# Turning the softmax weights of a cross-decoder in 32x32 squares on VectorE and through DRAM scratch, in place of TensorE transposes

## The chip, the cores and the metric

One NeuronCore of a Trainium2 chip runs the whole kernel. The metric is the time of one execution in microseconds (us) on the device.

## The reference, cut to what matters

The kernel computes a two-layer decoder trunk on 256 tokens of width 2048, all in float32. Layer one is a gated linear attention mixer and a gated convolutional FFN. Layer two is the cross-decoder: it makes keys and values from the output of layer one, attends to them and adds another FFN. With 256 tokens and blocks of 256 keys there is one block, so each query attends causally to all keys up to its own:

```python
kv = rms_norm(x, norm_w) @ w_kv
k, v = jnp.split(kv, 2, axis=-1)
k = rms_norm(k.reshape(B, S, H, Dh), k_norm_w)        # 16 heads of 128
v = v.reshape(B, S, H, Dh)
...
q = (rms_norm(q, q_norm_w) * (Dh ** -0.5)).transpose(0, 2, 1, 3)
...
s_own = jnp.einsum('bhqd,bhkd->bhqk', q_c, k_own)
s_own = s_own + bias_table[:, rel_bucket(dist_own)][None]
s_own = jnp.where(dist_own >= 0, s_own, -jnp.inf)
p = jax.nn.softmax(scores, axis=-1)
o = jnp.einsum('bhqk,bhkd->bhqd', p_own, v_own)
```

The softmax weights of a head are made with queries on partitions and keys along the free dimension. The product with the values needs them with keys on partitions, so they have to be turned.

## The kernel before

**Weights.** The kernel is a long row of matrix products against float32 weights that pass through once. `WeightStream` loads them in chunks of 128x2048 (1 MB) into three buffers `wraw` on SyncE's queue (L112). Each chunk is worked off in two halves of 128x1024: ScalarE rounds a half to `whi` (L132), VectorE subtracts to get the rest `wlo` (L133), and TensorE multiplies with both. There are four buffers each for `whi` and `wlo`; splits are issued two to three halves ahead. The next load is issued when a `wraw` buffer is free, that is after the L133 of the second half of an earlier chunk.

**Steps and jobs.** Each half is one `step()`. Side work is put in a list with `after(n, job)`, which lets `job` run before the n-th step from now. A scheduler then orders each engine's instructions; `tc.issue_after(x)` keeps an instruction behind x in that order. Each engine, SyncE's and GpSimd's DMA queues among them, goes through its instructions in order.

**The cross-decoder.** Q, K and V are each projected in four groups g of 8 halves (`gemm_tok`, L357 and L360), four heads per group; chunks of K are `w_kk`, of V `w_kv`. In the text, half n counts from the first half of K, so K has halves 0 to 31 and V 32 to 63. After a K group, `head_norm` squares and normalizes it (L917, L918 on ScalarE; L920, L921, L925 on VectorE; the power L923 on GpSimd) and `features` turns it for the scores (L933 on TensorE, L936 and L938 on ScalarE, L939 on VectorE). Then, per head, `softmax(hd)` multiplies the scores (L949, L951), adds the bias and takes the maximum (L958), exponentiates (L960) and scales (L962, L964). The three blocks of a head, queries 0 to 127 against keys 0 to 127 and queries 128 to 255 against both key tiles, stand side by side in one tile of 128x384. `turn(hd)` transposes the three blocks on TensorE into PSUM (L971, tile `pT`) and splits 256 columns of the result into `whi`-like and `wlo`-like parts for the exact product (`split`, L382 and L383) and copies the other 128 (L977). `values` multiplies with V (L434).

**Other users of the queues there.** `make_ahead` loads later weights (L314, `ahead<-w_dn`) on SyncE, adds and subtracts their parts on VectorE (L311, L312) and stores them on GpSimd's queue (L321, `tsum<-ahead`). `bias_rows` writes and reads a small scratch for the bias (`bscr`, L909). `turn_h` and `last_down` write and read `hscr`.

The jobs of a K group before the change:

```python
        for i in range(4):
            after(5 + i, lambda i=i, g=g: softmax(4 * g + i))
            after(7 + i, lambda i=i, g=g: turn(4 * g + i))
```

Of the kernel before, what the change touches and what calls it, by code (L numbers as in the profile page):

```python
# [8 lines left out]
F32 = mybir.dt.float32  # L9
# [16 lines left out]
MH = 16  # L26
# [119 lines left out]
def trunk(ctx: ExitStack, tc: tile.TileContext, xT, cst, msk, w1p, w2a, w_k, w_qa, w_v2, w_v, w_g, w_go,  # L146
          w_up0, w_dn0, w_kk, w_kv, w_mq, w_mo, w_up1, w_dn1, rel, onehot, out):
    nc = tc.nc
    V, A, T = nc.vector, nc.scalar, nc.tensor
# [9 lines left out]
    dram = ctx.enter_context(tc.tile_pool(name="dram", bufs=1, space=DRAM))  # L159

    def slot(shape, dt, name):
        return big.tile(shape, dt, name=name, tag="slot")
# [4 lines left out]
    def bank(name, shape):  # L167
        return mis_ps.tile(list(shape), F32, name=name, tag="bank")

    ws = WeightStream(tc, raw, parts)  # L170
# [4 lines left out]
    for layer, todo in enumerate(ahead):  # L175
        t = dram.tile([len(todo), 128, 2048], F32, name=f"tsum{layer}")
# [55 lines left out]
    ident = mk[:, 0:128]  # L232
# [70 lines left out]
    def after(steps, job):  # L303
        later.append((cur[0] + steps, job))
# [43 lines left out]
    def gemm_tok(xs, groups=1):  # L348
        out_ = [acc_ps.tile([128, 2, 512], F32, name="acc") for _ in range(groups)]
        for q0 in range(0, KT, 2):  # L350
            for ps in out_:
                hi, lo = step()
                for ks in ((0,), (1,)) if cur[0] < 3 and groups > 1 else ((0, 1),):
                    tiles_ = [(q0 + k, t, k * 512) for k in ks for t in range(2)]
                    for x0 in (0, S):
                        for kt, t, c in tiles_:
                            T.matmul(ps[:, t, :], xs(kt)[:, x0 + 128 * t:x0 + 128 * t + 128], hi[:, c:c + 512],  # L357
                                     start=kt == 0 and x0 == 0, stop=False)
                    for kt, t, c in tiles_:
                        T.matmul(ps[:, t, :], xs(kt)[:, 128 * t:128 * t + 128], lo[:, c:c + 512],  # L360
                                 start=False, stop=kt == KT - 1)
        ws.prefetch(cur[0])
        return out_ if groups > 1 else out_[0]
# [4 lines left out]
    def both(ps, name):  # L368
        t = temp(name)
        A.copy(t, ps[:, :, S:])  # L370
        V.tensor_add(t, t, ps[:, :, :S])
        return t
# [8 lines left out]
    def split(dst_hi, dst_lo, src):  # L381
        A.copy(dst_hi, src)  # L382
        V.tensor_sub(dst_lo, src, dst_hi.bitcast(F32))  # L383
# [37 lines left out]
    def v_out(v, ps, n):  # L421

        r0, r1 = (n.col[:, t:t + 1] for t in range(2))
        A.activation(v[0][:, 0, :], ps[:, 0, :], AF.Copy, scale=r0)
        V.scalar_tensor_tensor(v[0][:, 1, :], ps[:, 0, :], r0, v[0][:, 0, :].bitcast(F32),
                               op0=OP.mult, op1=OP.subtract)
        A.activation(v[1], ps[:, 1, :], AF.Copy, scale=r1)
# [80 lines left out]
    for hd in range(GH):  # L508
        ps = gemm(xs, KT)
        rstd = nrm.rstd  # L510
        k = both(ps, "k")
        V.tensor_mul(k, k, bc(rstd))
        b = bcum[hd]
# [64 lines left out]
    for hd in range(GH):  # L578
        ps = gemm(xs, KT)
        q = both(ps, "q")  # L580
# [11 lines left out]
    for hd in range(GH):  # L592
        for c in range(2):
            ps = gemm(xs, KT)
            g = both(ps, "g")
# [317 lines left out]
    def head_norm(ps, name):  # L913
        t_, sq = slot([128, 2, 512], F32, name), slot([128, 2, 512], F32, "hsq")
        for t in range(2):
            r = n_q.col[:, t:t + 1]
            A.activation(sq[:, t, :], ps[:, t, :], AF.Square, scale=r)  # L917
            A.activation(t_[:, t, :], ps[:, t, :], AF.Copy, scale=r)  # L918
        ss = small.tile([128, 8], F32, name="ss")
        V.tensor_reduce(ss, sq.rearrange("p t (h d) -> p (t h) d", d=128), axis=AX.X, op=OP.add)  # L920
        V.tensor_scalar(ss, ss, 1.0 / 128, EPS, op0=OP.mult, op1=OP.add)  # L921
        rr = small.tile([128, 8], F32, name="rr")
        nc.gpsimd.tensor_tensor(rr, ss, mhalf, op=OP.pow)  # L923
        u = t_.rearrange("p t (h d) -> p (t h) d", d=128)
        V.tensor_mul(u, u, rr[:, :, None].to_broadcast([128, 8, 128]))  # L925
        return t_

    def features(t_, c, f, scale, c0):

        tp = bank("tr", (128, 2, S))  # L930
        for i in range(2):
            for t in range(2):
                T.transpose(tp[:, i, 128 * t:128 * t + 128],  # L933
                            t_[:, t, (2 * c + i) * 128:(2 * c + i + 1) * 128], ident)
        whole, halves_ = f[0][:, 2 * c:2 * c + 2, :], f[1][c]
        A.activation(whole, tp[:, :, :128], AF.Copy, scale=scale)  # L936
        hi, lo = halves_[:, :, 0, :], halves_[:, :, 1, :]
        A.activation(hi, tp[:, :, c0:], AF.Copy, scale=scale)  # L938
        V.scalar_tensor_tensor(lo, tp[:, :, c0:], scale, hi.bitcast(F32), op0=OP.mult, op1=OP.subtract)  # L939

    qf, kf, ox = [], [], []
    pts = [None] * MH
    p0s, p1s = [], []

    def softmax(hd):
        (q0, q1), (k0, k1) = qf[hd // 4], kf[hd // 4]
        q1, k1 = q1[hd // 2 % 2][:, hd % 2], k1[hd // 2 % 2][:, hd % 2]
        sp = bank("s", (128, 384))
        T.matmul(sp[:, 0:128], q0[:, hd % 4, :], k0[:, hd % 4, :], start=True, stop=True)  # L949
        for i, (a, b) in enumerate(((0, 0), (0, 1), (1, 0))):  # L950
            T.matmul(sp[:, 128:384], q1[:, a, :], k1[:, b, :], start=i == 0, stop=i == 2)  # L951
        s = temp("s", (128, 384))
        st = small.tile([128, 4], F32, name="st")
        bt = bias[hd // 4][:, hd % 4, :]
        for t, (c0, c1) in enumerate(((0, 128), (128, 384))):
            n = c1 - c0
            rev = bass.AP(tensor=bt.tensor, offset=bt.offset + n - 1, ap=[bt.ap[0], [-1, n]])
            V.tensor_tensor_reduce(s[:, c0:c1], sp[:, c0:c1], rev, -1.0, 3.0e38, OP.add, OP.min,  # L958
                                   st[:, t:t + 1])
            A.activation(s[:, c0:c1], s[:, c0:c1], AF.Exp, bias=st[:, t:t + 1], scale=-1.0,  # L960
                         accum_out=st[:, 2 + t:3 + t])
        V.reciprocal(st[:, 2:4], st[:, 2:4])  # L962
        for t, (c0, c1) in enumerate(((0, 128), (128, 384))):
            V.tensor_scalar(s[:, c0:c1], s[:, c0:c1], st[:, 2 + t:3 + t], None, op0=OP.mult)  # L964
        pts[hd] = s

    def turn(hd):
        s = pts[hd]
        tp = bank("pT", (128, 384))
        for c in range(3):  # L970
            T.transpose(tp[:, 128 * c:128 * c + 128], s[:, 128 * c:128 * c + 128], ident)  # L971
        if hd % 8 == 0:
            p1s.append(slot([128, 8, 128], F32, "p1"))
        if hd % 2 == 0:
            p0s.append(slot([128, 2, 2, S], F32R, "p0"))
        split(p0s[-1][:, hd % 2, 0], p0s[-1][:, hd % 2, 1], tp[:, :256])
        A.copy(p1s[-1][:, hd % 8], tp[:, 256:])  # L977

    def values(v, p):
        op = bank("o", (128, 2, S))  # L980
        for i in range(2):
            hd = 2 * p + i
            p0 = p0s[p][:, i]
            mix(op[:, i, :], v, (hd % 4) * 128, p0[:, 0], p0[:, 1], p1s[hd // 8][:, hd % 8])
        o = slot([128, 2, 2 * S], F32R, "ox")
        split(o[:, :, :S], o[:, :, S:], op)
        ox.append(o)
# [7 lines left out]
    for g in range(4):  # L995
# [5 lines left out]
        f = (q8[:, g % 2 * 4:g % 2 * 4 + 4], (q1[:, 0:2], q1[:, 2:4]))  # L1001
# [4 lines left out]
    for g in range(4):  # L1006
        ps = gemm_tok(xs)
        t_ = head_norm(ps, "k")
        if g % 2 == 0:
            k8 = slot([128, 8, 128], F32, "k0")  # L1010
        f = (k8[:, g % 2 * 4:g % 2 * 4 + 4], [slot([128, 2, 2, S], F32R, f"k1{c}") for c in range(2)])
        kf.append(f)
        for c in range(2):
            after(3 + c, lambda t_=t_, c=c, f=f: features(t_, c, f, kqw, 0))
        for i in range(4):
            after(5 + i, lambda i=i, g=g: softmax(4 * g + i))
            after(7 + i, lambda i=i, g=g: turn(4 * g + i))
    for g in range(4):
        ps = gemm_tok(xs)
        if g % 2 == 0:  # L1020
            vm1 = slot([128, 2, 512], F32, "vm1")
        v = (slot([128, 2, 512], F32R, "vm0"), vm1[:, g % 2, :])
        v_out(v, ps, n_q)
        for c in range(2):
            after(1 + c, lambda v=v, p=2 * g + c: values(v, p))
# [116 lines left out]
```

## Time and profile before

| | us |
|---|---|
| median of 3 runs (2206.11 to 2206.84) | 2206.62 |
| the profiled execution, its own time | 2206.03 |
| span of its profile | 2204.2 |
| TensorE (PE) busy | 2197.5 |
| VectorE (DVE) busy | 1760.4 |
| ScalarE (ACT) busy | 1319.0 |
| GpSimd (POOL) busy | 88.5 |

PE is TensorE's matmul, PEld its weight load, SP SyncE; a "q" behind an engine's name is its queue of issued DMAs and waits. In rows of groups the last part gives busy time and the mean time of one in ns, then the idle time of the engine just before them and what ended it. Rows of the timeline start with start and length in us. Rows of windows give stretch, length, then busy time and number of instructions of PE, PEld, DVE, ACT and POOL, the granted clock of TensorE, the busy share of the 16 DMA engines and GB/s. DMA rows give the number of issues, KB each and the median us from issue to landing. Rows of waits give total us, times and the longest. Rows of queues give packets, MB and the share of the 16 engines' span that they took.

### The profile page before, as it was taken

To read this page: it belongs to the slowest core of one execution; us is meant where nothing else is said; L and a number is where in the kernel's file an instruction comes from. 1 tells how busy PE (TensorE), PEld (TensorE's weight loads), DVE (VectorE), ACT (ScalarE), POOL (GpSimd) and SP (SyncE) were. 2 spreads that over 40 slices of the span, in tenths; PEclk is the share of its full clock that TensorE was granted. 3 is DMA by queue.
4 is the path that set the end of the run, shared out by engine and by line. 5 is a ranking of instruction groups with operands and counts; after the bars stand their busy time and mean duration, and the time that the engine had idled before them with its cause. 6 is when DMAs were issued, how large, how long until landed. Compare 5 with 4: busy or idle time off the path is not lost.

```text
span 2204.2 us, 31059 instructions
## 1 busy us (share of the span) xinstructions
PE 2197.5 (100%) x11721; PEld 1899.7 (86%) x11721; DVE 1760.4 (80%) x2539; ACT 1319.0 (60%) x1848; POOL 88.5 (4%) x142
## 2 busy tenths in 40 slices
PE   9999999999999999999999999999999999999999
PEld 7889888888888888888888888888888888888887
DVE  6676877888888887877777777678888888878887
ACT  6655654656556565666656665446655665556565
POOL 0000000000000000000011100000000000000000
PEclk9999999999999999999999999999999999999999
DMA  7675678777777776887768666677777777878995
GB/s 288 211 264 206 235 272 300 265 266 274 271 270 268 278 273 216 296 326 298 279 239 301 243 219 244 224 265 265 267 272 273 273 269 278 290 258 314 321 374 207
DMA packets 91385, 592.41 MB, mean 269 GB/s; under 512 B 10673, under 2 KB 11201, under 8 KB 28514
## 3 DMA queue, kind: packets, MB, share of 16 engines
q1 hardware_dynamic: 75762, 512.69, 65.3%
q0 software_dynamic: 14896, 77.15, 9.1%
q8 instruction: 92, 1.51, 0.3%
q10 hardware_dynamic: 576, 0.58, 0.1%
q14 instruction: 59, 0.48, 0.1%
HBM read 522.99 MB, written 67.40 MB: 268 GB/s over the span
## 4 chain that ended last, share of the span: by engine, by line
PE 99%; DMA 0%; ACT 0%; DVE 0%; SPq 0%; issue 0%
PE acc L342 40%; PE acc L344 21%; PE acc L736 14%; PE acc L357 10%; PE p L736 6%; PE acc L360 5%; PE sT L548 0%; DMA wraw<-w_v 0%; PE tr L933 0%; PE s L951 0%; PE pT L971 0%; PE z L454 0%; PE oT L434 0%; PE s L949 0%; PE o L434 0%; PE hT L800 0%
## 5 line engine op out<-in xcount | busy, mean ns | idle before, releaser
L132 ACT CAST whi<-wraw 128x1024 fp32r<-128x1024 f32 (+1 forms) x786 | 798.5, 1020 | 633.4 <-PE acc L342 302.6
L133 DVE TENSOR_TENSOR wlo<-wraw,whi 128x1024 fp32r<-128x1024 f32 (+1 forms) x786 | 921.4, 1184 | 284.6 <-ACT whi L132 103.5
L342 PE MATMUL acc<-xw,whi 128*128 128x512 f32 x3328 | 796.4, 391 | 0.0
L342 PEld LDWEIGHTS acc<-xw,whi 128*128 128x128 f32 x3328 | 611.4, 188 | 117.5
L344 PEld LDWEIGHTS acc<-xw,wlo 128*128 128x128 f32 x3328 | 427.2, 191 | 16.2
L344 PE MATMUL acc<-xw,wlo 128*128 128x256 f32 x3328 | 433.5, 283 | 0.0
L736 PE MATMUL acc<-whi,hid 128*128 128x512 f32 x596 | 173.9, 390 | 0.0
L133 DVE TENSOR_TENSOR wlo<-ahead,whi 128x1024 fp32r<-128x1024 f32 x92 | 112.2, 1224 | 38.8 <-ACT whi L132 23.3
L357 PE MATMUL acc<-whi,xkv 128*128 128x512 f32 x512 | 132.7, 393 | 0.0
L736 PEld LDWEIGHTS acc<-whi,hid 128*128 128x128 f32 x596 | 111.5, 188 | 22.8
L357 PE MATMUL acc<-whi,xw 128*128 128x512 f32 x512 | 129.7, 393 | 1.4 <-ACT whi L132 1.4
L132 ACT CAST whi<-ahead 128x1024 fp32r<-128x1024 f32 x92 | 96.1, 1054 | 56.4 <-PE p L736 43.4
L736 PE MATMUL p<-whi,hid 128*128 128x512 f32 x386 | 124.8, 390 | 0.0
L357 PEld LDWEIGHTS acc<-whi,xw 128*128 128x128 f32 x512 | 95.2, 188 | 22.2 <-ACT whi L132 2.3
L357 PEld LDWEIGHTS acc<-whi,xkv 128*128 128x128 f32 x512 | 94.4, 188 | 18.2
L685 ACT ACTIVATE au<-up,cs 128x256 f32<-128x256 f32 x176 | 96.0, 593 | 7.9 <-DVE up L681 7.8
L687 DVE SCALAR_TENSOR_TENSOR au<-up,cs,au 128x255 f32<-128x255 f32 x176 | 83.4, 481 | 20.6 <-ACT au L685 20.5
L736 PE MATMUL acc<-wlo,hid 128*128 128x512 f32 x298 | 97.2, 389 | 0.0
L736 PE MATMUL acc<-whi,comb 128*128 128x512 f32 x320 | 95.6, 389 | 0.0
L736 PEld LDWEIGHTS p<-whi,hid 128*128 128x128 f32 x386 | 72.5, 188 | 15.1
L689 DVE SCALAR_TENSOR_TENSOR au<-up,cs,au 128x254 f32<-128x254 f32 x176 | 79.9, 478 | 0.0
L370 ACT COPY up<-acc 128x512 f32<-128x512 f32 x88 | 51.6, 586 | 46.4 <-PE acc L344 45.5
(267 smaller groups left out, 2199.0 us busy)
## 6 DMA issues: line engine op xcount, KB each, us to landing
wraw<-w_up SPq DMA_DIRECT2D x176, 1024.0 KB, 5.1
ahead<-w_dn SPq DMA_DIRECT2D x53, 1024.0 KB, 9.3
tsum<-ahead POOLq DMA_DIRECT2D x53, 1024.0 KB, 7.7
ahead<-tsum SPq DMA_DIRECT2D x46, 1024.0 KB, 6.5
wraw<-w_dn SPq DMA_DIRECT2D x53, 768.0 KB, 6.1
wraw<-w_dn SPq DMA_DIRECT2D x35, 1024.0 KB, 5.4
wraw<-w_g SPq DMA_DIRECT2D x16, 1024.0 KB, 5.3
wraw<-w_go SPq DMA_DIRECT2D x16, 1024.0 KB, 6.6
```

Source lines behind the costliest of these rows:

```text
L132: nc.scalar.copy(hi[:, a:b], src[:, a:b])
L133: self.low = nc.vector.tensor_sub(lo[:, a:b], src[:, a:b], hi[:, a:b].bitcast(F32))
L342: T.matmul(ps[:, b, :], two[i][0][:, c:c + 128], xs(kt), start=kt == 0, stop=False)
L344: T.matmul(ps[:, b, :S], two[i][1][:, c:c + 128], xs(kt)[:, :S], start=False, stop=kt == kts - 1)
L357: T.matmul(ps[:, t, :], xs(kt)[:, x0 + 128 * t:x0 + 128 * t + 128], hi[:, c:c + 512], start=kt == 0 and x0 == 0, stop=False)
L360: T.matmul(ps[:, t, :], xs(kt)[:, 128 * t:128 * t + 128], lo[:, c:c + 512], start=False, stop=kt == KT - 1)
L370: A.copy(t, ps[:, :, S:])
L685: A.activation(au[:, i, :], t[:, i, :], AF.Identity, bias=col(cb + n), scale=col(cw + 2 * 2 * FT + n))
L687: V.scalar_tensor_tensor(au[:, i, 1:], t[:, i, :S - 1], col(cw + 2 * FT + n), au[:, i, 1:], op0=OP.mult, op1=OP.add)
L689: V.scalar_tensor_tensor(au[:, i, 2:], t[:, i, :S - 2], col(cw + n), au[:, i, 2:], op0=OP.mult, op1=OP.add)
L736: T.matmul(p[n], x[xi], w[wi][:, 512 * f:512 * f + 512], start=n not in begun, stop=left[n] == 0)
```

## The change

`turn` no longer uses TensorE. VectorE transposes the 128x384 tile in squares of 32x32, each in its own place. Four DMAs on SyncE's queue, one for each 32 partitions, write the squares to a DRAM scratch `turned`, each to the place that its square has in the transposed matrix, in runs of 32 numbers (128 bytes). One DMA on GpSimd's queue reads the head's three transposed blocks back into SBUF, 3 runs of 512 bytes on each partition. The split and the copy move into a job of their own, `weights(hd)`, four steps after `turn`, and read the tile from SBUF. The writes are ordered behind the last weight load that was issued, and the transpose behind the last L133. `turn`'s tile now comes from the pool of general slots, not from PSUM.

```diff
+    turned = dram.tile([MH, 12, 32, 128], F32, name="turned")
+
     def turn(hd):
-        s = pts[hd]
-        tp = bank("pT", (128, 384))
-        for c in range(3):
-            T.transpose(tp[:, 128 * c:128 * c + 128], s[:, 128 * c:128 * c + 128], ident)
+
+        t = slot([128, 2, 384], F32, "pT")
+        with tc.issue_after(ws.low.ins):
+            V.transpose(t[:, 0], pts[hd])
+        to = turned[hd].rearrange("f b (m a) -> m b f a", a=32)
+        for m in range(4):
+            with tc.issue_after(ws.load.ins):
+                nc.sync.dma_start(to[m], t[32 * m:32 * m + 32, 0].rearrange("b (f a) -> b f a", a=32))
+        nc.gpsimd.dma_start(t[:, 1].rearrange("k (j q) -> k j q", j=3),
+                            turned[hd].rearrange("(j f) b q -> (f b) j q", f=4))
+        pts[hd] = t[:, 1]
+
+    def weights(hd):
+        tp = pts[hd]
         if hd % 8 == 0:
             p1s.append(slot([128, 8, 128], F32, "p1"))
         if hd % 2 == 0:
...
             after(5 + i, lambda i=i, g=g: softmax(4 * g + i))
             after(7 + i, lambda i=i, g=g: turn(4 * g + i))
+            after(11 + i, lambda i=i, g=g: weights(4 * g + i))
```

With the lines that the change adds, the transpose stands at L973 of the changed kernel, the writes at L977, the read at L978 and the copy of the 128 columns at L989.

## The prediction

> **What bounds the kernel now.** I read the page's busy shares and chain first, then PE's waits over the whole span.
>
> ```profile
> span 2204.2 us, 31059 instructions
> PE 2197.5 (100%) x11721; PEld 1899.7 (86%) x11721; DVE 1760.4 (80%) x2539; ACT 1319.0 (60%) x1848; POOL 88.5 (4%) x142
> PE 99%; DMA 0%; ACT 0%; DVE 0%; SPq 0%; issue 0%
> PE acc L357 <- ACT whi L132: 1.4, 2, 0.9
> ```
>
> PE is busy for 2197.5 of 2204.2 us, the chain that ended last is PE for 99%, and the longest wait of PE on another engine is 1.4 us in all. So a TensorE instruction that goes shortens the kernel by what it occupied, and a new wait of PE lengthens it one to one. Next I looked at the place of the change, the K and V projections, in PE's timeline and in the changed line's own view.
>
> ```profile
> L971 PE MATMUL pT<-mk,s x48: 270/272/277, 1241.5 to 1372.4; 128*128 128x128 f32 x48
> ...
> 1249.11 0.38 PE L949 MATMUL s<-k,q 128*128 128x128 f32 x2
> 1249.25 0.60 PE L951 MATMUL s<-k,q 128*128 128x256 f32 x3
> 1249.69 0.85 PE L360 MATMUL acc<-wlo,xkv 128*128 128x512 f32 x3
> 1250.38 1.98 PE L357 MATMUL acc<-whi,xkv 128*128 128x512 f32 x8
> 1252.19 1.07 PE L360 MATMUL acc<-wlo,xkv 128*128 128x512 f32 x4
> 1253.10 1.98 PE L357 MATMUL acc<-whi,xkv 128*128 128x512 f32 x8
> 1254.91 0.85 PE L360 MATMUL acc<-wlo,xkv 128*128 128x512 f32 x3
> 1255.60 0.49 PE L971 MATMUL pT<-mk,s 128*128 128x128 f32 x3
> 1255.84 0.47 PE L360 MATMUL acc<-wlo,xkv 128*128 128x512 f32 x1
> 1256.16 2.00 PE L357 MATMUL acc<-whi,xkv 128*128 128x512 f32 x8
> ```
>
> Twelve matmuls work off one half of a weight chunk. Such a half without transposes lasts from 1250.38 to 1253.10, 2.72 us; the next, with three, from 1253.10 to 1256.16, 3.06 us. Three transposes cost PE 0.34 us, not three times their 272 ns, since matmuls overlap. One head's scores cost it 0.58 us (1249.11 to 1249.69).
>
> **The change: what goes.** 48 transposes, 16 heads at 0.34 us: 5.4 us off the path. [...]
>
> **What comes on DVE.** One 32x32-square transpose of 128x384 per head. No row shows it; its neighbours:
>
> ```profile
> L133 DVE TENSOR_TENSOR wlo<-wraw,whi 128x1024 fp32r<-128x1024 f32 x53 | 64.8, 1223 | 33.8 <-ACT whi L132 28.2 <-PE acc L360 3.4 <-ACT p L382 2.0
> L958 DVE CUSTOM_DVE_ANT_0 s<-s,bias 128x256 f32<-128x256 f32 x16 | 6.7, 420 | 0.0
> L383 DVE TENSOR_TENSOR p<-pT,p 128x256 fp32r<-128x256 f32 x16 | 6.6, 418 | 1.7 <-ACT p L382 1.7
> L939 DVE SCALAR_TENSOR_TENSOR k<-tr,kqw,k 128x512 fp32r<-128x512 f32 x8 | 6.0, 750 | 3.3 <-ACT k L938 3.1 <-PE acc L357 0.2
> L964 DVE TENSOR_SCALAR s<-s,st 128x256 f32<-128x256 f32 x16 | 5.6, 348 | 0.0
> L964 DVE TENSOR_SCALAR s<-s,st 128x128 f32<-128x128 f32 x16 | 4.6, 290 | 0.4
> L958 DVE CUSTOM_DVE_ANT_0 s<-s,bias 128x128 f32<-128x128 f32 x16 | 4.5, 284 | 0.8 <-PE s L951 0.8
> L920 DVE TENSOR_REDUCE ss<-hsq 128x8 f32<-128x1024 f32 x3 | 3.7, 1219 | 0.9 <-ACT hsq L917 0.9
> L925 DVE TENSOR_TENSOR k<-k,rr 128x1024 f32<-128x1024 f32 x3 | 3.7, 1218 | 0.1
> L132 ACT CAST whi<-wraw 128x1024 fp32r<-128x1024 f32 x52 | 54.8, 1053 | 40.5 <-PE acc L357 30.4 <-issue 6.0 <-ACT s L960 1.4
> ```
>
> From L964 at 256 columns (0.35 us) to L939 at 512 (0.75 us); I take 0.5, 8 us for 16 heads. Is it covered? In the changed program's order PE no longer spreads the heads over its halves 14 to 58 of these projections, but does four per K group of 8 halves: scores at halves 14, 16, 23, 25, 31, 33, 40 and 42. In a group DVE has 8 splits x 1.22 = 9.8 us, four heads at 0.42 + 0.28 + 0.35 + 0.29 + 0.42 and about 0.3 of small ones, with the transpose 0.5: 10.2, L920 and L925 2.4, two of L939 1.5, some three sums of the weights ahead near 2: 25.9 us of durations. PE's group is 8 x 2.72, four scores at 0.58 and the eight transposes of the key features, 0.9 at the rate above: 25.0. Durations of neighbours overlap (the PE rows show it: 1.98 us every 1.81), so I take 24 of 25.0 us: covered, but with little to spare. DVE does its splits three halves ahead, some 7 us, which this may eat up.
>
> **What comes on ACT.** The same copies, now read from SBUF: nothing, within 0.1 us a head either way, under the 30.4 us that the casts wait for PE.
>
> **What comes on the queues.** SP gets 64 writes of 32x12 runs of 128 bytes, POOL 16 reads back, in order with what stands there. Behind a write on SP stands the next weight load; behind a read on POOL the power of L923 and the sums' stores.
>
> ```profile
> SPq L112 <- DVE wlo L133: 129.6, 22, 7.4
> 2.12 1.38 SPq L112 DMA_DIRECT2D wraw<-w_v  x3
> L909 POOL DMA_DIRECT2D bias<-bscr x4: 748/760/798, 1154.8 to 1159.7; - x4
> L923 POOL TENSOR_TENSOR rr<-ss,mhalf x8: 1637/1911/2678, 1131.3 to 1322.6; 128x8 f32<-128x8 f32 x8
> wraw<-w_kk SPq DMA_DIRECT2D x16, 1024.0 KB, 5.8
> bias<-bscr POOLq DMA_DIRECT2D x4, 512.0 KB, 9.7
> hscr<-hT POOLq DMA_DIRECT2D x8, 256.0 KB, 4.4
> res<-hscr POOLq DMA_DIRECT2D x8, 256.0 KB, 5.3
> bscr<-brow POOLq DMA_DIRECT2D x1, 24.0 KB, 2.8
> ```
>
> Issue: three loads in a row take 1.38 us, 0.46 each. 64 x 0.46 = 29 us of SP in the 94 us that PE needs for halves 14 to 44 (30 x 2.72, 16 x 0.58 of scores and 3 x 0.9 of features). SP is mostly waiting for a free weight buffer there (129.6 us from 1225 to 1390), so this hides. Weight loads also have slack: a buffer comes round every 3 x 5.44 = 16.3 us, of which landing takes 5.8 and working off two halves 2.72 + 1.05 + 1.22 = 5.0; 5.5 us are left, and the casts run ahead besides, so I allow 10 us once for a late weight. DVE's transposes stand in its order so that a write is ready just before the load behind it; SP is not held by them.
>
> Round trip of a head: four issues 1.8, landing 2.8 to 4.4 (the small and the larger store of scratch), POOL's issue 0.76, landing 5.3 to 9.7: 10.7 to 16.7 us. Room: the tightest is head 2, turned near PE half 17, whose copy stands on ACT before the features that PE needs at half 23: 6 x 2.72 + 1.1 - 2.9 for ACT's work behind it = 14.5 us. L923 of the second K group stands behind head 1's read; it starts some 5 us before PE misses it. At the middle, 13.7 us, it all hides.
>
> **DMA engines.** Here the change could run out of room.
>
> ```profile
> 1260.00:1280.00 20.00, 20.00 (x101) 16.69 (x101) 12.71 (x25) 11.51 (x23) 0.00 (x0) 1.00 0.71 263
> 1280.00:1300.00 20.00, 20.00 (x99) 16.70 (x98) 14.98 (x33) 12.32 (x25) 3.09 (x2) 1.00 0.78 275
> 1300.00:1320.00 20.00, 20.00 (x103) 16.92 (x102) 15.25 (x32) 11.22 (x22) 0.53 (x1) 1.00 0.51 170
> 1320.00:1340.00 20.00, 20.00 (x99) 16.60 (x98) 14.26 (x25) 13.01 (x26) 1.66 (x1) 1.00 0.80 291
> q1 hardware_dynamic: 75762, 512.69, 65.3%
> q10 hardware_dynamic: 576, 0.58, 0.1%
> ```
>
> Their DMA share (the last column but one) is 0.70 in the mean: 66 of 94 us, 28 free. The reads are 16 x 196 KB; q1 moves a packet of 6.77 KB in 0.653 x 16 x 2204 / 75762 = 0.304 us, 45 ns per KB, so they take 9 us of each engine. The writes are 64 x 384 runs, 1536 on each engine. One costs at least its bytes, 6 ns; at most what the small packets of q10 cost (1 KB in the mean), 0.001 x 16 x 2204 / 576 = 61 ns. Less the bytes' 45 that is 16 + 6 = 22 ns, with a share rounded so that it may be half. I take 12, since q1's packets show no fixed part: 18 us, 93 of 94 with the rest. So it just fits; no wait of PE is taken, and 0.4 us for odd ones.
>
> **The sum.** The profiled execution took 2206.03 us (span 2204.2 and 1.8 around it), 0.6 under the median 2206.62. 2206.0 - 5.4 + 0.4 = 2201.0, and with the median's 0.6: 2201.6 us.
>
> **Rivals.** (a) The DMA engines become the bound: slower. Each ns per run is 1.5 us. With 28 free, 9 for reads and 10 us of slack, it decides from 29 / 1.536 = 19 ns a run. At 30 ns: 46 + 9 - 38 = 17 us of late weights, less 5.4: 2218; at 61 ns: 94 + 9 - 38 - 5.4 = 60, 2266. For it: shares of 0.7 to 0.8 already, and the heads drawn together. Against: q1's rate. [...]
>
> (b) The round trip takes the upper end, 16.7 us: ACT stands before the copy, the features come late and PE waits 2.2 us in each of three groups, 6.6 us: 2206.6 - 5.4 + 6.6 = 2207.8, no change. For it: the bias read's 9.7 us; against it: the 4.4 and 5.3 of the other scratch. DVE, full for 24 of 25.0 us, would show the same size.
>
> (c) PE gains each transpose's full duration, 48 x 0.272 = 13.1 us: 2206.6 - 13.1 + 0.4 = 2193.9. The timeline's 0.34 us for three speaks against it.
>
> **The numbers.** Forecast 0.38, (a) 0.38, (b) 0.22, (c) 0.02. About 0.2%, 4.4 us, is what a measurement of this kernel can tell from no change. The forecast and (c) are faster by more, 0.40; (b) is within, 0.22; (a) is slower, 0.38. The range leaves out (c) and (a) from 34 ns a run on, to which I give 0.17: from 2200 (1.2 us more than the sum, if three transposes cost PE 0.42 us) to 2224. The forecast's own range is 2200 to 2202.
>
> **What would show it.** Right: L971 gone, PE's longest waits in these projections under 1 us, halves of 2.72 us throughout, DMA share near 0.95 between halves 14 and 44, landing of weights below 9 us. Wrong by (a): landing of w_kv over 11 us, ACT's casts waiting for DMA, PE for whi. Wrong by (b): ACT waiting before the copies of p for the read back, PE for the features or scores. A write's issue on SP over 1 us would break the queue's part of the sum.

## The result, and the profile after

| | median us (lowest to highest, runs) | against before, 95% interval |
|---|---|---|
| before, beside it | 2206.39 (2206.04 to 2206.84, 15) | |
| changed | 2209.97 (2206.96 to 2216.38, 15) | 1.0019 [1.0013, 1.0026] |

The change makes the kernel 0.2% slower, where 0.2% faster was forecast. Its runs also differ by up to 9.4 us, those of before by 0.8 us. The profiled execution took 2206.96 us, which is the shortest of the changed kernel's runs; a second profile, further down, was taken of an execution near the median of its runs.

The page of the changed kernel, its span, busy times and SyncE's DMA queue:

```profile
span 2204.9 us, 31147 instructions
...
PE 2193.6 (99%) x11673; PEld 1895.5 (86%) x11673; DVE 1765.2 (80%) x2555; ACT 1318.2 (60%) x1848; POOL 100.0 (5%) x158
...
q1 hardware_dynamic: 101362, 515.84, 66.3%
```

PE works 3.9 us less than before (2197.5), yet the span is 0.7 us longer: some 4.6 us are new idle time. The waits of PE over the whole span (us in total, times, longest) say where:

```profile
PE o L431 <- ACT vm L424: 3.9, 1, 3.9
PE acc L357 <- ACT whi L132: 2.0, 2, 1.3
```

One wait of 3.9 us was not there before: the product with the values stands still for `vm`, the features of the second V group, which `v_out` makes on ScalarE (L424). That line has nothing to do with the weights that were turned. The timelines of the same stretch show why it is late (start, length, engine; in brackets the idle time before and what ended it). Head 14 is the subject:

```profile
1329.54 0.57 DVE L973 STREAM_TRANSPOSE pT<-s 128x384 f32<-128x384 f32 x1
...
1332.10 8.68 SPq L977 DMA_DIRECT2D turned<-pT  x8
...
1340.78 1.07 PE L360 MATMUL acc<-wlo,xkv 128*128 128x512 f32 x4
...
1342.28 0.76 POOL L978 DMA_DIRECT2D pT<-turned  x1 [8.30 <-DMA turned<-pT]
...
1347.13 0.39 PE L357 MATMUL acc<-whi,xkv 128*128 128x512 f32 x1
...
1350.13 0.40 ACT L382 CAST p<-pT 128x256 fp32r<-128x256 f32 x1 [6.46 <-DMA pT<-turned]
1350.45 0.29 ACT L989 COPY p<-pT 128x128 f32<-128x128 f32 x1
1350.64 0.68 ACT L424 ACTIVATE vm<-acc,col_h 128x512 fp32r<-128x512 f32 x1
...
1351.38 0.58 PE L431 MATMUL o<-p,vm 128*128 128x256 f32 x1 [3.86 <-ACT vm L424]
```

VectorE turns the squares at 1329.5. The eight writes of heads 14 and 15 take SyncE from 1332.1 to 1340.8 to issue. GpSimd waits 8.3 us for head 14's writes and issues the read at 1342.3; ScalarE can copy it at 1350.1, 20.6 us after the transpose. ScalarE stands idle for 6.5 us before that copy. The last product that `vm` is made from, L360 of half 47, ends at 1341.9, and ScalarE is idle from 1343.7; it could make `vm` then, but `vm` is behind the copy in its order. TensorE goes on with the next V group until 1347.5 and needs `vm` next.

The wait costs more than its length, as the windows around it show (stretch, length, PE, PEld, DVE, ACT, POOL, granted clock, DMA share, GB/s):

```profile
1334.00:1347.40 13.40, 13.40 (x60) 10.87 (x58) 6.64 (x9) 3.97 (x7) 1.51 (x2) 1.00 0.97 294
1347.40:1350.80 3.40, 0.12 (x1) 0.00 (x0) 0.23 (x1) 0.67 (x3) 0.00 (x0) 1.00 1.01 392
1350.80:1354.30 3.50, 2.92 (x9) 2.54 (x10) 2.95 (x5) 3.49 (x6) 0.00 (x0) 0.51 0.49 201
1354.30:1358.00 3.70, 3.70 (x26) 3.35 (x25) 3.27 (x5) 1.89 (x3) 0.57 (x1) 1.00 0.37 75
```

After the wait TensorE has a granted clock of 0.51 for 3.5 us. The stall stands at the end of a stretch with a DMA share of 0.97 to 1.01.

The new instructions by line (ns least, median, most; then first and last start):

```profile
L973 DVE STREAM_TRANSPOSE pT<-s x16: 532/572/580, 1238.4 to 1331.1; 128x384 f32<-128x384 f32 x16
...
L977 SPq DMA_DIRECT2D turned<-pT x64: 302/497/3121, 1239.0 to 1340.3; - x64
...
L978 POOL DMA_DIRECT2D pT<-turned x16: 755/758/792, 1245.2 to 1343.3; - x16
```

A transpose takes 0.57 us, and an issue of a write on SyncE up to 3.1 us (0.50 in the median). How long the transfers take from issue to landing, in the median, stands in the DMA rows:

```profile
turned<-pT SPq DMA_DIRECT2D x64, 48.0 KB, 4.2
...
pT<-turned POOLq DMA_DIRECT2D x16, 192.0 KB, 5.2
```

In the median neither is slow. Three of the four windows that the prediction showed of before, now of the changed kernel, behind a longer one of 94 us:

```profile
1224.00:1318.00 94.00, 94.00 (x467) 79.44 (x466) 78.71 (x165) 62.06 (x127) 17.41 (x18) 1.00 0.87 272
1260.00:1280.00 20.00, 20.00 (x101) 16.94 (x100) 18.88 (x46) 13.77 (x32) 4.34 (x4) 1.00 0.91 304
1280.00:1300.00 20.00, 20.00 (x102) 17.02 (x101) 16.68 (x40) 15.72 (x39) 2.09 (x3) 1.00 0.84 272
1300.00:1320.00 20.00, 20.00 (x98) 16.82 (x98) 15.85 (x32) 10.94 (x19) 4.80 (x5) 1.00 0.96 285
```

The DMA share rises from 0.71, 0.78 and 0.51 to 0.91, 0.84 and 0.96.

### The profile page after: what moved, and what is told of

It reads as the page before. It is cut to its first block, busy times and chain, and to the rows that moved or that the text cites. A ratio compares the mean times of both kernels' runs of the same rounds, so it can differ in the third digit from the quotient of the medians.

```text
span 2204.9 us, 31147 instructions
## 1 busy us (share of the span) xinstructions
PE 2193.6 (99%) x11673; PEld 1895.5 (86%) x11673; DVE 1765.2 (80%) x2555; ACT 1318.2 (60%) x1848; POOL 100.0 (5%) x158
## 3 DMA queue, kind: packets, MB, share of 16 engines
q1 hardware_dynamic: 101362, 515.84, 66.3%
## 4 chain that ended last, share of the span: by engine, by line
PE 98%; DMA 1%; issue 0%; ACT 0%; SPq 0%; DVE 0%; POOL 0%; POOLq 0%
PE acc L342 40%; PE acc L344 21%; PE acc L736 14%; PE acc L357 10%; PE p L736 6%; PE acc L360 5%; PE sT L548 0%; DMA pT<-turned 0%; DMA wraw<-w_v 0%; DMA turned<-pT 0%; PE tr L933 0%; PE s L951 0%; PE z L454 0%; PE o L434 0%; PE oT L434 0%; PE s L949 0%
## 5 line engine op out<-in xcount | busy, mean ns | idle before, releaser
L133 DVE TENSOR_TENSOR wlo<-wraw,whi 128x1024 fp32r<-128x1024 f32 (+1 forms) x786 | 919.9, 1182 | 268.3 <-ACT whi L132 89.8
L133 DVE TENSOR_TENSOR wlo<-ahead,whi 128x1024 fp32r<-128x1024 f32 x92 | 112.2, 1223 | 38.2 <-ACT whi L132 22.3
L687 DVE SCALAR_TENSOR_TENSOR au<-up,cs,au 128x255 f32<-128x255 f32 x176 | 83.2, 480 | 20.7 <-ACT au L685 20.6
```

The source lines that it names most:

```text
L133: self.low = nc.vector.tensor_sub(lo[:, a:b], src[:, a:b], hi[:, a:b].bitcast(F32))
L687: V.scalar_tensor_tensor(au[:, i, 1:], t[:, i, :S - 1], col(cw + 2 * FT + n), au[:, i, 1:], op0=OP.mult, op1=OP.add)
```

## The experiments

**Theory A:** the transposes were worth about what was forecast, and the gain is given back because copies of the turned weights stand in ScalarE's order ahead of instructions that TensorE needs soon, and such a copy waits for a late read. **Theory B:** the DMA engines are full and weights land late. **Theory C:** VectorE is overloaded. **Theory D:** there was less to win.

The first four kernels ran beside one another, with before at 2206.38 us (28 runs).

**no_turn**, before without the transposes:

```diff
-        tp = bank("pT", (128, 384))
-        for c in range(3):
-            T.transpose(tp[:, 128 * c:128 * c + 128], s[:, 128 * c:128 * c + 128], ident)
+        tp = s
```

> The kernel before without its 48 transposes: the copies of p read s directly, so the turning of the weights is left out of the computation. Theory A (the transposes were worth what the clusters of before show, 16 x 0.35 us, and the changed kernel gives it back in waits) says 5.7 us under before, 2200.7 us. Theory D (part of the transposes lay in gaps that stay, so there was less to win) says 3 us or less, 2203.5 us or more.

Measured: 2200.64 us (2199.92 to 2201.0), ratio 0.9974 [0.9963, 0.9984], 5.7 us under before. D falls.

**squares_only**, the changed kernel without its DMAs:

```diff
-        to = turned[hd].rearrange("f b (m a) -> m b f a", a=32)
-        for m in range(4):
-            with tc.issue_after(ws.load.ins):
-                nc.sync.dma_start(to[m], t[32 * m:32 * m + 32, 0].rearrange("b (f a) -> b f a", a=32))
-        nc.gpsimd.dma_start(t[:, 1].rearrange("k (j q) -> k j q", j=3),
-                            turned[hd].rearrange("(j f) b q -> (f b) j q", f=4))
-        pts[hd] = t[:, 1]
+        pts[hd] = t[:, 0]
```

> The changed kernel without its 80 DMAs: the copies of p read the turned squares where VectorE left them, so the squares are not put in place. Theory A says VectorE's 16 instructions of about 0.5 us are hidden: as no_turn within 0.4 us, 2200.7 us. Theory C (VectorE, at 24 of 25 us per K group, is what the change overloads) says 2203 to 2207 us, with waits of TensorE for q, k or s.

Measured: 2200.73 us (2200.39 to 2201.21), ratio 0.9974 [0.9964, 0.9984]. Its page has a span of 2199.1 us and

```profile
PE 2191.8 (100%) x11673; PEld 1894.4 (86%) x11673; DVE 1765.7 (80%) x2555; ACT 1319.5 (60%) x1848; POOL 89.1 (4%) x142
```

VectorE does all its new work (1765.7 us against 1760.4 of before) and it costs nothing: C falls. What is lost comes with the DMAs.

**traffic_aside**, before with the squares, writes and reads added into a tile that nobody uses:

```diff
     def turn(hd):
         s = pts[hd]
+        t = slot([128, 2, 384], F32, "spare")
+        with tc.issue_after(ws.low.ins):
+            V.transpose(t[:, 0], s)
...
+        nc.gpsimd.dma_start(t[:, 1].rearrange("k (j q) -> k j q", j=3),
+                            turned[hd].rearrange("(j f) b q -> (f b) j q", f=4))
         tp = bank("pT", (128, 384))
```

> The kernel before, transposes on TensorE and all, plus the 16 transposes by VectorE, the 64 writes and the 16 reads into a tile that nobody uses. Theory A says the traffic by itself costs nothing, because only a copy of p that waits for its read holds anything up: before's 2206.4 us, within 0.6 us. Theory B (the DMA engines are full, weights land late, TensorE waits for them) says 2210 to 2216 us, as far above before as the changed kernel's runs lie above 2200.7 us.

Measured: 2206.29 us (2206.14 to 2207.09), ratio 1.0000 [0.9991, 1.0009]. The page's queue row, and then the longest wait of PE on another engine:

```profile
q1 hardware_dynamic: 101362, 515.84, 66.2%
```

```profile
PE acc L357 <- ACT whi L132: 1.6, 2, 1.1
```

The same 101362 packets as in the changed kernel, and no new wait. The heads stand further apart here, as in before (the transposes run from 1237.6 to past 1359, in the changed kernel from 1238.4 to 1331.1), so this shows the price of the traffic but not of its bunching; all_late, below, has the bunching too.

**behind_vm**, the changed kernel with the copies of heads 14 and 15 behind the second V group's features:

```diff
+        vms.append((A.activation(v[1], ps[:, 1, :], AF.Copy, scale=r1).ins, low.ins))
...
+        with ExitStack() as late:
+            if hd > 13:
+                for ins in vms[-1]:
+                    late.enter_context(tc.issue_after(ins))
             split(p0s[-1][:, hd % 2, 0], p0s[-1][:, hd % 2, 1], tp[:, :256])
...
-            after(11 + i, lambda i=i, g=g: weights(4 * g + i))
+            after((20 if 4 * g + i > 13 else 11) + i, lambda i=i, g=g: weights(4 * g + i))
```

> The changed kernel, with the copies of the weights of heads 14 and 15 ordered behind the features of the second V group on ScalarE and VectorE; their transposes, writes and reads stay where they are. Theory A (the gain is lost because ScalarE stands in front of head 14's copy while TensorE waits for those features, 3.9 us, and runs at half clock for 3.4 us after it) says the wait goes and the time is 2200.7 to 2202 us. Theory B (full DMA engines, late weights) says no change, 2207 to 2212 us.

Measured: 2204.91 us (2201.67 to 2208.18), ratio 0.9993 [0.9985, 1.0002]. Against the changed kernel's 2209.97 that is 5 us back, but A had promised 2200.7 to 2202. The waits of PE no longer name `vm`, but there is another (lines were added, so the key features stand at L940 and L941, the scores at L951):

```profile
PE s L951 <- DVE k L941: 1.8, 1, 1.8
```

The timeline of ScalarE and TensorE at that place:

```profile
1281.04 0.41 ACT L382 CAST p<-pT 128x256 fp32r<-128x256 f32 x1 [5.68 <-DMA pT<-turned]
1283.72 0.41 ACT L382 CAST p<-pT 128x256 fp32r<-128x256 f32 x1 [2.07 <-DMA pT<-turned]
...
1285.55 0.68 ACT L940 ACTIVATE k<-tr,kqw 128x512 fp32r<-128x512 f32 x1
...
1287.86 0.49 PE L951 MATMUL s<-k,q 128*128 128x128 f32 x2 [1.81 <-DVE k L941]
```

And a window behind it:

```profile
1289.50:1291.20 1.70, 1.70 (x6) 1.31 (x5) 1.70 (x3) 0.00 (x0) 0.00 (x0) 0.50 0.98 407
```

It is the same thing with another victim: the copies of heads 4 and 5 wait for their reads, the key features come behind them (with a cast, its split and one sum of later weights in between), and TensorE waits 1.8 us for these. Here too the clock is at half afterwards. So one place was mended, and there are several.

The next three ran together, with before at 2206.44 us (2205.64 to 2209.31, 22 runs).

**all_late** does it for every head:

```diff
+        marks.append((A.activation(v[1], ps[:, 1, :], AF.Copy, scale=r1).ins, low.ins))
...
+        marks.append((exp.ins, mul.ins))
         pts[hd] = s
...
+        with ExitStack() as late:
+            for ins in marks[-1]:
+                late.enter_context(tc.issue_after(ins))
...
-            after(11 + i, lambda i=i, g=g: weights(4 * g + i))
+            after((17 if g < 3 else 18) + i // 2, lambda i=i, g=g: weights(4 * g + i))
```

> The changed kernel with the copies of every head's weights moved to step 17 or 18 after its K group and ordered, on ScalarE and VectorE, behind the last softmax piece or V features that stand there, so that no feature, exponential or V feature of the next group is queued behind a copy that waits for its read. Writes and reads stay. Theory A (the whole loss is the queueing behind late reads) says 2200.7 to 2201.7 us, and a spread of the runs under 2 us. Theory B2 (a late read also costs in another way: tiles held longer, a write behind a weight load, a weight that lands late) says 2203 us or more.

Measured: 2200.56 us (2200.16 to 2200.65), ratio 0.9972 [0.9960, 0.9983]: 5.9 us under before, as fast as no_turn, and its 6 runs lie within 0.5 us. Its page:

```profile
span 2198.9 us, 31134 instructions
...
PE 2192.2 (100%) x11673; PEld 1895.0 (86%) x11673; DVE 1764.6 (80%) x2555; ACT 1318.8 (60%) x1848; POOL 100.3 (5%) x158
```

Its waits of PE, all of them:

```profile
PE acc L357 <- ACT whi L132: 1.4, 2, 0.8
PE junk L205 <- POOL idle L202: 1.3, 1, 1.3
```

And head 14 in the timelines of GpSimd and ScalarE (the read stands at L981, the V features at L426 and L429, the copy of the 128 columns at L995):

```profile
1340.07 0.76 POOL L981 DMA_DIRECT2D pT<-turned  x1 [7.97 <-DMA turned<-pT]
...
1341.24 0.68 ACT L426 ACTIVATE vm<-acc,col_h 128x512 fp32r<-128x512 f32 x1
...
1345.52 0.68 ACT L429 ACTIVATE vm<-acc,col_h 128x512 f32<-128x512 f32 x1
...
1348.79 0.30 ACT L995 COPY p<-pT 128x128 f32<-128x128 f32 x1 [2.21 <-DMA pT<-turned]
```

Head 14's read is no quicker: issued at 1340.1 after 8 us of waiting for its writes, copied 8.7 us later. From its first write to the landing of its read it needs 18.8 us, in the changed kernel 18.0. Only `vm` now goes ahead of the copy. ScalarE still waits 2.2 us for the read, and TensorE does not wait for ScalarE there: it takes up `vm` at 1346.2, 2.6 us before the copy. The tiles held longer cost nothing either, and a weight that lands late does not: one row of all waits between 1190 and 1420 is

```profile
ACT whi L132 <- DMA wraw<-w_kv: 6.7, 2, 4.0
```

and no wait of TensorE comes of it. So B2 falls with B.

**later_only** gives the copies more room than the changed kernel does, without the ordering (in all_late they are asked for up to three steps later still):

```diff
-            after(11 + i, lambda i=i, g=g: weights(4 * g + i))
+            after(15 + i, lambda i=i, g=g: weights(4 * g + i))
```

> The changed kernel with the copies asked for four steps later (15 to 18 in place of 11 to 14) and nothing ordered by hand. The list of ScalarE's instructions still has some copies ahead of the features: the first three for heads 8 and 9 before the exponentials of the next group, head 14's last copy before the second V features. Theory A (order decides, not only room) says between behind_vm and all_late: 2201 to 2205 us, with a spread of 2 us or more. A theory of room alone (four more steps of 2.7 us are 11 us, more than any read was late) says 2200.7 us.

Measured: 2207.88 us (2205.76 to 2211.42), ratio 1.0006 [0.9997, 1.0015]. Room alone would have given 2200.7, and A's 2201 to 2205 was too low as well. A wait of PE and ScalarE's timeline before it:

```profile
PE o L431 <- ACT vm L424: 5.0, 1, 5.0
```

```profile
1351.40 0.30 ACT L989 COPY p<-pT 128x128 f32<-128x128 f32 x1 [6.82 <-DMA pT<-turned]
1351.61 0.68 ACT L424 ACTIVATE vm<-acc,col_h 128x512 fp32r<-128x512 f32 x1
```

One copy of head 14 stands ahead of `vm` again, as the expectation had read from the list. A single copy of 0.3 us that waits 6.8 us for its read is enough for TensorE's wait of 5.0 us.

**after_again**, the changed kernel once more:

> The changed kernel once more, beside the others on one chip, for a second profile and the spread of its runs. Theory A says a median of 2208.5 to 2211.5 us, runs that lie 5 us or more apart, and in the profile TensorE waiting for ScalarE (vm, k or o) each time behind a copy of p that waits for its read, with a lower granted clock after each wait; the waits and the clock's share sum to the distance from 2200.7 us.

Measured: 2211.27 us (2207.72 to 2215.75), ratio 1.0021 [1.0012, 1.0030]; its profiled execution took 2211.6 us, with a span of 2209.6. From its page, and then its waits of PE:

```profile
PE 2196.4 (99%) x11673; PEld 1897.9 (86%) x11673; DVE 1765.0 (80%) x2555; ACT 1317.7 (60%) x1848; POOL 99.5 (5%) x158
```

```profile
PE o L431 <- ACT vm L424: 4.3, 1, 4.3
PE acc L357 <- ACT whi L132: 1.9, 2, 1.1
PE s L949 <- DVE st L958: 1.8, 1, 1.8
```

The slower execution has the wait for `vm` again, 4.3 us, and a second one of 1.8 us. That one goes through VectorE, where the expectation had named ScalarE alone, as the timeline shows:

```profile
1321.03 0.41 ACT L382 CAST p<-pT 128x256 fp32r<-128x256 f32 x1 [3.92 <-DMA pT<-turned]
1321.47 0.42 DVE L383 TENSOR_TENSOR p<-pT,p 128x256 fp32r<-128x256 f32 x1 [2.15 <-ACT p L382]
1321.81 0.28 DVE L958 CUSTOM_DVE_ANT_0 s<-s,bias 128x128 f32<-128x128 f32 x1
...
1322.50 0.57 PE L949 MATMUL s<-k,q 128*128 128x128 f32 x2 [1.81 <-DVE st L958]
```

The low part of head 10's copy (L383) stands ahead of the bias step of the next scores (L958), and TensorE waits to go on. The windows around it:

```profile
1320.60:1322.50 1.90, 0.09 (x1) 0.00 (x0) 0.98 (x5) 0.60 (x2) 0.00 (x0) 1.00 0.51 209
1322.50:1324.00 1.50, 1.50 (x7) 1.40 (x8) 0.68 (x2) 1.12 (x5) 0.00 (x0) 0.59 0.03 11
1324.00:1326.00 2.00, 2.00 (x6) 1.60 (x5) 2.00 (x6) 2.00 (x7) 0.21 (x1) 0.50 0.18 25
```

TensorE idles for 1.8 us and then runs at 0.59 and 0.50 of its clock. What a profile has over all_late's span of 2198.9 us is the growth of PE's waits plus the growth of its busy time (over 2192.2). At half clock matmuls kept TensorE busy for longer (four of L360 take 1.91 us at 1324.4 in after_again, 1.07 elsewhere). Half of the time that TensorE worked at half clock by the traces' clock records is 1.5, 4.4, 2.8 and 1.7 us for the four rows, close to the growth of their busy time:

| kernel | PE's waits, all_late's 2.7 taken off | busy time over all_late's | sum | span over all_late's |
|---|---|---|---|---|
| changed, first profile | 4.7 | 1.4 | 6.1 | 6.0 |
| changed, after_again | 6.6 | 4.2 | 10.8 | 10.7 |
| later_only | 5.3 | 3.1 | 8.4 | 8.5 |
| behind_vm | 2.2 | 1.6 | 3.8 | 3.8 |

The two columns have to add up to the span, so the sums show where the loss lies and not why. Why is shown by all_late: with the same DMAs and no quicker read, another order of the copies removes the loss. Not tried: which part of the traffic makes head 14's round trip the longest. That its writes land just after the reads of heads 12 and 13 (1339.7 and 1340.4, the writes from 1340.7), and that one issue on SyncE stretches to 3.1 us meanwhile, is read from the trace of the changed kernel and not tested.

## Why the prediction was wrong

**What goes: right.** 5.4 us were forecast for the 48 transposes; no_turn shows 5.7. Rival (c), which priced each transpose at its full duration, 13.1 us in all, falls.

**VectorE: right.** 0.5 us taken for a transpose, 0.57 measured, and covered: squares_only is as fast as no_turn (2200.73 and 2200.64 us). It had room on the average (busy for 80% of the span), though in after_again it passes a late copy on to L958.

**ScalarE's copies: right as work** (in the median 0.41 and 0.29 us in the changed kernel, where before's from PSUM took 0.37 and 0.27; no_turn and squares_only, which read them from SBUF, run at 2200.64 and 2200.73 us), wrong as a place in its order, below.

**SyncE's issues: the price failed, the conclusion held.** 0.46 us each was forecast, and an issue of over 1 us was named as what would break this part; the longest took 3.1 us, eight took 8.7, and all 64 add up to 47.6 us where 29 were forecast. SyncE was also held by the transposes, 8.7 us in four waits, where the prediction had it not held. The weight loads behind were not late enough to matter, for TensorE never waits for `whi` between 1225 and 1400 in the profile of the changed kernel.

**DMA engines, and rival (a): "just fits" was right.** The packet records of the changed kernel's trace give the 24576 runs of 128 bytes 12.8 ns in the mean, 19.7 us on each engine, where 12 ns were taken and 19 were (a)'s point. That this came so close is in part luck: 12 was picked between bounds of 6 and 22 because q1's packets show no fixed part, which one mean of all sizes cannot show. Over the 94 us from 1224 to 1318 the DMA share is 0.87, where 93 of 94 us were forecast, in part because heads 12 to 15 write only after that. With (a) at 0.38, the prediction gave the same chance as its own forecast to something that traffic_aside (2206.29 us, before beside it 2206.38) and all_late (2200.56) price at nothing.

**The round trip: the step that failed.** Two of its terms were too small. The landing of a head's writes was bounded at 2.8 to 4.4 us by stores that had stood alone, and the four issues at 1.8 us; for head 14 the four issues took 5.1 us, the first write landed 8.6 us after its issue, and both together, from the first write at 1332.1 to the read's issue at 1342.3, took 10.2 us. The mean fitted, 12.5 us over the 16 heads from the first write to the landing of the read, but the heads come in bunches, and in the last bunch the DMA engines are at 0.97 to 1.01. With the read, head 14 took 18.0 us from its first write, past the upper bound of 16.7, while head 0 needed 6.2 (1239.0 to 1245.2) and a landing of some 5 us.

**The room: the other half of it.** The prediction looked for the tightest copy in front of K's features and named head 2 with 14.5 us. It did not look at what else stands behind a copy in ScalarE's order: V's features (head 14, in both profiles of the changed kernel), and on VectorE the bias step of the next scores. Head 2 never showed. Head 14's own room was much like the 14.5: from its first write at 1332.1 to 1347.5, less the 1.25 us from its copy to TensorE's next product, are 14.2 us, and 18.0 less 14.2 is the wait. There the round trip alone failed. But in behind_vm head 5 needed 13.2 us, less than the forecast's middle of 13.7, and TensorE still waited 1.8 us, so that its room was some 11.4: the tightest place was not found either.

**The sum: 0.4 us "for odd waits" was the mis-sized term.** In its place stand 4.7 and 6.6 us of waits and 1.4 and 4.2 us of slow clock. This is the mechanism of rival (b), held at 0.22, with ScalarE before a copy as its sign; (b) gave 2207.8 from three equal waits of 2.2 us, and it was one or two waits at other places, plus the clock, which no case priced: 2209.97. That this lies inside the stated 2200 to 2224 is luck: the range reached so far up for (a), which did not come, and the forecast's own range was 2200 to 2202. With the copies ordered, all_late's 2200.56 lies in that one, so the rest of the sum held.

## What to carry to other kernels

Replacing work on the bound engine by a detour through memory paid here only once nothing that the bound engine needs soon was queued behind the consumer of the detour. So list, for every engine that consumes it, what comes next in its order, and order the consumer behind all of that where its own deadline is far; here that turned 4.8 us lost (after_again, against before beside it) into 5.9 us won (all_late) without making head 14's transfers faster. Bound a transfer's latency by its worst bunch (head 14's 18.0 us, where the mean of the heads was 12.5), not by a transfer that stood alone or by the mean share of the DMA engines, and treat a kernel whose runs spread more than before as one that may have a wait that timing decides (9.4 us of spread in the changed kernel, 0.5 in all_late).

## What the runs showed of the hardware that was not expected

Each of the five waits of TensorE of 1.8 us or more in these traces cost more than itself. After 3.9 us the granted clock was 0.51 for 3.5 us; after only 1.8 us it was 0.59 and 0.50 for the next 3.5 us (after_again) and 0.50 in the window shown of behind_vm. After 4.3 us it stayed low for longer; TensorE went on at 1354.9 in after_again, and this window is still at half:

```profile
1357.50:1360.00 2.50, 2.50 (x10) 2.21 (x10) 2.26 (x4) 0.35 (x1) 0.00 (x0) 0.50 0.00 0
```

The clock records of the traces have stretches of 3.41 us at half in the first profile of the changed kernel and after both waits of 1.8 us, and of 6.83 us after the waits of 4.3 and 5.0 us (later_only). So waits of 1.8 us were followed by as long a slow stretch as the wait of 3.9 us, and those of 4.3 and 5.0 us by one twice as long. What starts a slow stretch and what ends it no run here isolates.

A DMA's issue on SyncE, 0.3 us at the least, took up to 3.1 us, though the instruction moved the same 48 KB. Head 14's four took 0.38, 0.87, 0.54 and 3.12 us between 1332.1 and 1337.2, so the full engines of that stretch alone do not explain it; the cause stays open.
